# Attention weights of four heads turned together, and their sums with the values one piece later

## The chip, the cores and the metric

The kernel runs on one core of a Trainium2 chip. A time is the device time of one execution in microseconds (us); the kernel before was timed in three runs. One execution was also recorded instruction by instruction; times inside it count from the start of its span, the stretch from its first to its last instruction. Engines: TensorE (PE, matrix products; PEld is its loading of the stationary operand), VectorE (DVE), ScalarE (ACT), GpSimd (POOL), and SyncE (SP), which issues the loads of the weights.

## The reference

A decoder of two layers on 256 tokens of width 2048, all in float32. Layer 0 mixes by a state-space recurrence, layer 1 by attention; each is followed by a gated feed-forward part. The change touches the attention alone: 32 query heads of 64 columns, eight of them sharing one of four key/value heads, tokens in two blocks of 128, and each query sees at most the last 128 tokens:

```python
s = jnp.einsum('bnqhgd,bnkhd->bnhgqk', q, kw) * (HEAD_DIM ** -0.5)
s = s - slopes * dist
s = jnp.where(valid[None, :, None, None], s, -jnp.inf)
m = jnp.maximum(jnp.max(s, axis=-1, keepdims=True), sink)
p = jnp.exp(s - m)
p = p / (jnp.sum(p, axis=-1, keepdims=True) + jnp.exp(sink - m))
o = jnp.einsum('bnhgqk,bnkhd->bnqhgd', p, vw).reshape(bsz, seq, Q_DIM)
return (o @ w_o)
```

## The kernel before

**The large products.** Each weight matrix is read in blocks of 512 x 512, and each block is split into a high part (ScalarE, L122) and a low part (VectorE, L127). A *piece* (`piece`, with `products` at L922 to L924) multiplies one such block with the activations of 256 tokens: four quarters `a`, two token tiles `t`, three matmuls each (high x high, high x low, low x high), 24 matmuls into two accumulators named acc. `linear` runs the four pieces of one result of 512 columns. A piece asks for the weights that come three blocks later to be split, and for loads two further ahead.

**Work between pieces.** The list `slots` holds other work. After every piece `linear` takes the next entry of `slots` and issues all that is in it. Instructions go to their engines in the order that a scheduler chooses ahead of time: it follows the order of the code by priority, and puts later instructions of an engine ahead where it reckons that the earlier ones would wait. [...]

**Attention.** `attention` first computes keys and values (kv), then for each of four chunks c of eight heads the queries (a `linear`). `heads(c, q)` gives three functions for the chunk, each working on groups g4 of four heads:

- `turn_q` transposes the queries on TensorE (L1153) and copies them out.
- `scores(g4)` computes the scores of four heads (L1165 for the first token block, 128 columns; L1166 for the second, 256 columns), adds the slopes on VectorE (L1169), takes the maxima (L1170, L1171), exponentiates on ScalarE (L1181) and divides by the sums (L1187). A head's weights are 128 rows of 384 columns of the tile sc.
- `values(g4)` does for each head i: three transposes of 128 x 128 into one bank (L1197), a copy of that bank to the tile pT, on VectorE for even i and on ScalarE for odd i (L1199), and three matmuls with the values (L1208 to L1210) into half of a bank po: partitions 0 to 63 for an even head, 64 to 127 for an odd one. The sums of head i are issued after the transposes of head i + 1. After each odd head the bank is split into the high part (ScalarE, L1214) and the low part (VectorE, L1215) of oT, the left operand of the out-projection.

There are eight banks of matmul output (`ps`, bufs=8); `bank` takes one, for acc as for all tiles named here. pT has three buffers.

The slots of a chunk c are filled when its queries are issued, and worked off during the four pieces of the next `linear`: after the first piece turn_q, the second group's values of the chunk before, and scores(0); then scores(1); then values(0); then nothing. For chunk 3 they are worked off during the first eight pieces of the out-projection (order `O_ORDER`: its blocks of rows 0, 1, 2 for two accumulators each, then block 3 for both): turn_q with the late values and scores(0); scores(1); nothing; values(0); values(1). Block q of the out-projection reads the tile oT of chunk q, which is complete once both groups' values are done; block 3 is read from the seventh piece on.

## Time and profile before

| what | value |
|---|---|
| median of three runs | 2031.78 us (2030.18 to 2032.72) |
| the recorded execution | 2030.9 us |
| its span | 2029.1 us |
| TensorE busy in the span | 1984.3 us, 98% |
| VectorE, ScalarE busy | 1088.9 us, 860.1 us |
| mean granted TensorE clock | 0.993 |
| first to last start of a matmul with the values (L1208) | 1099.5 to 1230.0 us |

A line of a group of instructions reads: line in the code, engine, operation, tiles written <- tiles read, shapes, count | busy us, mean ns of one | idle us of that engine just before them, and what ended that idle time. A line of the timeline reads: start, duration, engine, line, operation, tiles, count, and in brackets the idle time ahead of it with what ended it; several of a kind are merged. Matmuls are pipelined, so their durations overlap, and one float32 matmul is recorded as one or two passes. "128*64" ahead of a shape is the part of TensorE's array (rows*columns) that the instruction uses.

### The profile page before, as it was taken

The page shows a single profiled execution, that of the slowest core. Times are in us where ns is not written, and L with a number is a line of the kernel's source. Part 1 is how long each engine was busy: PE and PEld are TensorE (multiplying, and loading weights), DVE is VectorE, ACT ScalarE, POOL GpSimd, SP SyncE. Part 2 cuts the span into 40 slices and gives each one's busy share as a digit, 9 for nine tenths or more (in the row PEclk, how much of TensorE's full clock was granted, in tenths as well). Part 3 has the DMA queues.
Part 4 walks back from the last instruction along what each step waited for, and adds up shares of the span by engine and source line. Part 5 has one row for each costly group of instructions (what it writes and reads, how often), then busy time and mean ns, then how long its engine had stood idle before and what let it go on. Part 6 is the DMA issues. An engine that isn't in the chain of part 4 may idle for free.

```text
span 2029.1 us, 25100 instructions
## 1 busy us (share of the span) xinstructions
PE 1984.3 (98%) x10640; PEld 1638.7 (81%) x10640; DVE 1088.9 (54%) x1343; ACT 860.1 (42%) x871; POOL 103.7 (5%) x77
## 2 busy tenths in 40 slices
PE   7699999999999999999999999999999999999998
PEld 6578888888888888888887778888888888888886
DVE  8955454445544544454567775544454445444445
ACT  6554444443344334333445454544333343334333
POOL 6850000000000000000000000000000000000000
PEclk9899999999999999999999999999999999999999
DMA  4037666565555655556555334556555655555564
GB/s 128 23 111 233 198 198 194 186 194 192 187 188 188 199 193 187 187 192 200 178 191 166 106 125 146 186 188 193 194 192 187 188 191 193 195 186 188 190 201 148
DMA packets 183317, 360.62 MB, mean 178 GB/s; under 512 B 10403, under 2 KB 10467, under 8 KB 183077
## 3 DMA queue, kind: packets, MB, share of 16 engines
q1 hardware_dynamic: 182192, 355.56, 54.4%
q8 instruction: 83, 1.36, 0.3%
q10 hardware_dynamic: 580, 2.14, 0.3%
q0 software_dynamic: 432, 1.33, 0.2%
q14 instruction: 30, 0.24, 0.0%
HBM read 356.90 MB, written 2.10 MB: 177 GB/s over the span
## 4 chain that ended last, share of the span: by engine, by line
PE 91%; DVE 6%; ACT 1%; DMA 1%; issue 1%; POOL 0%; DVEq 0%; ACTq 0%
PE acc L922 29%; PE acc L924 29%; PE acc L923 28%; DVE scan L573 1%; DVE w L127 1%; PE tr L1061 1%; DVE V L578 1%; DVE V L576 1%; DMA raw<-in_s_w_glu_dram 1%; PE pv L210 1%; PE tr L966 1%; PE po L1208 1%; PE tr L1197 0%; PE py L798 0%; ACT sc L1181 0%
## 5 line engine op out<-in xcount | busy, mean ns | idle before, releaser
L127 DVE TENSOR_TENSOR w<-raw,w 128x2048 fp32r<-128x2048 f32 x330 | 757.1, 2295 | 828.3 <-ACT w L122 828.3
L122 ACT ACTIVATE w<-raw 128x2048 fp32r<-128x2048 f32 x332 | 636.2, 1916 | 979.4 <-PE acc L924 873.6
L922 PE MATMUL acc<-w,xT 128*128 128x512 f32 x1568 | 612.8, 391 | 0.0
L924 PE MATMUL acc<-w,xT 128*128 128x512 f32 x1568 | 611.3, 390 | 0.0
L923 PE MATMUL acc<-w,xT 128*128 128x512 f32 x1568 | 610.6, 389 | 0.0
L924 PEld LDWEIGHTS acc<-w,xT 128*128 128x128 f32 x1568 | 294.3, 188 | 62.2 <-issue 1.0
L922 PEld LDWEIGHTS acc<-w,xT 128*128 128x128 f32 x1568 | 294.4, 188 | 61.3 <-issue 1.3
L923 PEld LDWEIGHTS acc<-w,xT 128*128 128x128 f32 x1568 | 294.4, 188 | 60.7 <-issue 0.5
L922 PE MATMUL acc<-w,hT 128*128 128x512 f32 x704 | 275.2, 391 | 0.0
L923 PE MATMUL acc<-w,hT 128*128 128x512 f32 x704 | 273.6, 389 | 0.0
L924 PE MATMUL acc<-w,hT 128*128 128x512 f32 x704 | 273.4, 389 | 0.0
L922 PEld LDWEIGHTS acc<-w,hT 128*128 128x128 f32 x704 | 132.1, 188 | 28.0 <-ACT hT L1063 1.2
L924 PEld LDWEIGHTS acc<-w,hT 128*128 128x128 f32 x704 | 132.1, 188 | 27.8
L923 PEld LDWEIGHTS acc<-w,hT 128*128 128x128 f32 x704 | 132.2, 188 | 27.0
L923 PE MATMUL acc<-w,gt 128*128 128x512 f32 x256 | 99.8, 390 | 0.6 <-DVE w L127 0.6
L922 PE MATMUL acc<-w,gt 128*128 128x512 f32 x256 | 100.1, 392 | 0.0
L924 PE MATMUL acc<-w,gt 128*128 128x512 f32 x256 | 99.7, 389 | 0.0
L923 PEld LDWEIGHTS acc<-w,gt 128*128 128x128 f32 x256 | 48.1, 188 | 10.6 <-DVE w L127 1.0
L924 PEld LDWEIGHTS acc<-w,gt 128*128 128x128 f32 x256 | 48.1, 188 | 10.1
L922 PEld LDWEIGHTS acc<-w,gt 128*128 128x128 f32 x256 | 48.1, 188 | 9.9
L1088 DVE TENSOR_TENSOR h<-h,acc 128x512 f32<-128x512 f32 x64 | 43.3, 686 | 23.7 <-PE acc L924 23.7
L1074 ACT ACTIVATE act<-acc,ry 128x512 f32<-128x512 f32 x44 | 30.1, 690 | 59.9 <-PE acc L924 59.9
(242 smaller groups left out, 1233.1 us busy)
## 6 DMA issues: line engine op xcount, KB each, us to landing
raw<-in_ffn_w_gate_dram SPq DMA_DIRECT2D x88, 1024.0 KB, 5.2
raw<-in_ffn_w_up_dram SPq DMA_DIRECT2D x88, 1024.0 KB, 5.2
raw<-in_ffn_w_down_dram SPq DMA_DIRECT2D x88, 1024.0 KB, 5.1
raw<-in_s_w_glu_dram SPq DMA_DIRECT2D x32, 1024.0 KB, 5.3
raw<-in_attn_w_qkv_dram SPq DMA_DIRECT2D x20, 1024.0 KB, 5.2
raw<-in_attn_w_o_dram SPq DMA_DIRECT2D x16, 1024.0 KB, 5.1
xk<-in_x_dram SPq DMA_DIRECT2D x4, 512.0 KB, 7.4
h<-in_x_dram SPq DMA_DIRECT2D x8, 256.0 KB, 5.6
```

What stands on the lines that cost most here:

```text
L122: keep(S.activation(w[:, 0], self.raw[i], AF.Copy))
L127: keep(e.tensor_tensor(lo, self.raw[i], hi.bitcast(F32), op=ALU.subtract))
L210: return (lambda *a, **k: pin(f(*a, **k))) if self.on else f
L573: keep(V.tensor_tensor(t_, ws[..., part], bc(Vt[hf][:, k - 1, :, part], 1, 2), op=ALU.mult))
L576: V.tensor_tensor(v, v, t_[:, 0], op=ALU.add)
L578: V.tensor_tensor(v, v, t_[:, 1, ::-1], op=ALU.add)
L922: keep(PE.matmul(acc, x_[:, 0], w[0][:, a], start=first, stop=False))
L923: PE.matmul(acc, x_[:, 0], w[1][:, a], start=False, stop=False)
L924: PE.matmul(acc, x_[:, 1], w[0][:, a], start=False, stop=last)
L966: PE.transpose(pt[:, t], h[t][:, kt * P : (kt + 1) * P], ident)
L1074: S.activation(s, pg[t], AF.Silu, scale=r[0][:, t : t + 1])
L1088: V.tensor_tensor(hc, hc, acc[t], op=ALU.add)
```

## The change

`values` is cut in two. `turned_s(g4)` transposes the weights of all four heads and copies them to four pT tiles (four buffers now, three before). `values(g4)` does only the sums, pair by pair of heads: a pair has one bank, and each of the three matmuls is issued first for the even head (partitions 0 to 63) and then for the odd one (64 to 127) before the next of the three.

The slots of a chunk become: after the first piece turn_q, turned_s of the second group of the chunk before, and scores(0); then values of that second group, and scores(1); then turned_s(0); then values(0). For chunk 3 two more slots follow, turned_s(1) and values(1); the empty slot there goes, so that values(1) comes after the sixth piece of the out-projection, where it came after the fifth.

```diff
-                def values(g4):
-                    s = st[g4]
-                    po = {}
-
-                    def turned(i):
+                def turned_s(g4):
+
+                    st["pT"] = []
+                    for i in range(4):
                         pt = bank([P, 3, P], "tr")
                         for b3 in range(3):
-                            PE.transpose(pt[:, b3], s[:, i, b3 * P : (b3 + 1) * P], ident)
-                        pT = ap.tile([P, 3, P], F32, tag="pT", name=nm("pT"), bufs=3)
+                            PE.transpose(pt[:, b3], st[g4][:, i, b3 * P : (b3 + 1) * P], ident)
+                        pT = ap.tile([P, 3, P], F32, tag="pT", name=nm("pT"), bufs=4)
                         (S.copy if i % 2 else V.tensor_copy)(pT, pt)
-                        return pT
...
-                    before = None
-                    for i in range(4):
-                        pT = turned(i)
-                        if before:
-                            weighted(*before)
-                        before = (i, pT)
-                    weighted(*before)
...
+                        st["pT"].append(pT)
+
+                def values(g4):
+
+                    v0, v1 = (kv[:, t, 256 + HD * c : 256 + HD * c + HD] for t in range(2))
+                    for i2 in range(2):
+                        po = bank([P, 2, P], "po")
+                        hs = [(po[e * HD : (e + 1) * HD], st["pT"][2 * i2 + e]) for e in range(2)]
+                        for o, pT in hs:
+                            PE.matmul(o[:, 0], v0, pT[:, 0], start=True, stop=True)
+                        for o, pT in hs:
+                            PE.matmul(o[:, 1], v0, pT[:, 1], start=True, stop=False)
+                        for o, pT in hs:
+                            PE.matmul(o[:, 1], v1, pT[:, 2], start=False, stop=True)
+                        a = 2 * g4 + i2
+                        v = po.rearrange("p t q -> p (t q)")
+                        S.copy(ot[c][:, 0, a], v)
+                        V.tensor_tensor(ot[c][:, 1, a], v, ot[c][:, 0, a].bitcast(F32), op=ALU.subtract)
...
-                turn_q, scores, values = heads(c, q)
-                slots.append([turn_q, *late, partial(scores, 0)])
-                slots.append([partial(scores, 1)])
-                if c == 3:
-                    slots.append([])
+                turn_q, scores, turned_s, values = heads(c, q)
+                slots.append([turn_q, *late[:1], partial(scores, 0)])
+                slots.append([*late[1:], partial(scores, 1)])
+                slots.append([partial(turned_s, 0)])
                 slots.append([partial(values, 0)])
-                late = [partial(values, 1)]
-                slots.append(late if c == 3 else [])
-
+                late = [partial(turned_s, 1), partial(values, 1)]
+            slots.extend([f] for f in late)
```

More of the change, by code (lines that the diff above doesn't have):

```diff
@@ L1199, in turned @@
                         (S.copy if i % 2 else V.tensor_copy)(pT, pt)
-                        return pT
-                    def weighted(i, pT):
-                        if i % 2 == 0:
-                            po[i // 2] = bank([P, 2, P], "po")
-                        rows = slice(i % 2 * HD, (i % 2 + 1) * HD)
-                        o = po[i // 2][rows]
-                        v0, v1 = (kv[:, t, 256 + HD * c : 256 + HD * c + HD] for t in range(2))
-                        PE.matmul(o[:, 0], v0, pT[:, 0], start=True, stop=True)
-                        PE.matmul(o[:, 1], v0, pT[:, 1], start=True, stop=False)
-                        PE.matmul(o[:, 1], v1, pT[:, 2], start=False, stop=True)
-                        if i % 2:
-                            a = 2 * g4 + i // 2
-                            v = po[i // 2].rearrange("p t q -> p (t q)")
-                            S.copy(ot[c][:, 0, a], v)
-                            V.tensor_tensor(ot[c][:, 1, a], v, ot[c][:, 0, a].bitcast(F32), op=ALU.subtract)
@@ L1217, in values @@
-                    before = None
-                    for i in range(4):
-                        pT = turned(i)
-                        if before:
-                            weighted(*before)
-                        before = (i, pT)
-                    weighted(*before)
-                return turn_q, scores, values
+                        st["pT"].append(pT)
[14 more added lines that the diff above has]
+                        V.tensor_tensor(ot[c][:, 1, a], v, ot[c][:, 0, a].bitcast(F32), op=ALU.subtract)
@@ L1227, in attention @@
+                return turn_q, scores, turned_s, values
             late = []
```

## The prediction

> **What bounds the kernel now.** I read the page first (busy time, the chain that ended last, the costliest groups), then the windows of the attention stage, then its groups by line, and last the timeline of TensorE alone, matmul by matmul. Two engines' lines and the chain settle the bound:

> ```profile
> PE 1984.3 (98%) x10640; PEld 1638.7 (81%) x10640; DVE 1088.9 (54%) x1343; ACT 860.1 (42%) x871; POOL 103.7 (5%) x77
> ...
> PE 91%; DVE 6%; ACT 1%; DMA 1%; issue 1%; POOL 0%; DVEq 0%; ACTq 0%
> L122 ACT ACTIVATE w<-raw 128x2048 fp32r<-128x2048 f32 x332 | 636.2, 1916 | 979.4 <-PE acc L924 873.6
> ```

> TensorE (PE) is busy nearly throughout and is 91% of the chain. The splitting of weights on ScalarE (L122) idles 979.4 us, 873.6 of it until a TensorE matmul gives a buffer back: weights wait for TensorE, not TensorE for weights. So a microsecond off TensorE's stream in the attention stage should come off the end, as long as nothing else becomes late there. In that stage VectorE (DVE) is the next engine. One query chunk c lasts exactly 37.16 us, from its first q transpose to the next chunk's:

> ```profile
> 1112.40:1149.56 37.16, 36.05 (x210) 27.98 (x208) 27.88 (x65) 18.96 (x48) 0.00 (x0) 1.00 0.34 114
> ```

> (columns: PE, PEld, DVE, ACT, POOL busy, then TensorE's granted clock, the DMA share, GB/s). VectorE is busy 27.88, ScalarE 18.96; the granted clock is 1.00 and the DMA share 0.34, so neither clock nor loads matter here.

> **What the touched instructions cost.** The groups by line over 1096 to 1231 us, where all the weighted sums with the values lie:

> ```profile
> L1197 PE MATMUL tr<-ident,sc 128*128 128x128 f32 x96 | 15.1, 281 | 0.0
> L1208 PE MATMUL po<-pT,kv 128*64 128x128 f32 x64 | 12.9, 298 | 4.0 <-DVE pT L1199 4.0
> L1215 DVE TENSOR_TENSOR oT<-po,oT 128x256 fp32r<-128x256 f32 x15 | 6.2, 415 | 9.5 <-ACT oT L1214 9.5
> L1214 ACT CAST oT<-po 128x256 fp32r<-128x256 f32 x16 | 5.9, 368 | 21.1 <-PE po L1210 21.1
> ```

> There are 96 transposes (32 heads of three) and, of each of the three matmuls of a head, 64 passes, that is two passes per matmul, six per head. Durations overlap in the pipeline, so I cost by starts. A matmul into acc starts every 0.23 us (three steps from 1133.33 to 1134.02, below); whatever lies between two of them beyond 0.23 is what the inserted work costs. The third group of four heads, on TensorE alone:

> ```profile
> 1132.21 0.39 PE L924 MATMUL acc<-w,xT 128*128 128x512 f32 x1
> 1132.44 0.82 PE L1197 MATMUL tr<-ident,sc 128*128 128x128 f32 x6
> 1133.02 0.47 PE L922 MATMUL acc<-w,xT 128*128 128x512 f32 x1
> 1133.33 0.39 PE L923 MATMUL acc<-w,xT 128*128 128x512 f32 x1
> ...
> 1134.02 0.39 PE L923 MATMUL acc<-w,xT 128*128 128x512 f32 x1
> 1135.52 0.43 PE L1208 MATMUL po<-pT,kv 128*64 128x128 f32 x2 [1.11 <-DVE pT L1199]
> ...
> 1137.89 0.48 PE L924 MATMUL acc<-w,xT 128*128 128x512 f32 x1
> 1138.21 0.39 PE L922 MATMUL acc<-w,xT 128*128 128x512 f32 x1
> ...
> 1139.60 0.39 PE L922 MATMUL acc<-w,xT 128*128 128x512 f32 x1
> 1139.92 0.43 PE L1208 MATMUL po<-pT,kv 128*64 128x128 f32 x2
> 1140.19 0.38 PE L1209 MATMUL po<-pT,kv 128*64 128x128 f32 x2
> 1140.40 0.38 PE L1210 MATMUL po<-pT,kv 128*64 128x128 f32 x2
> 1140.72 0.50 PE L923 MATMUL acc<-w,xT 128*128 128x512 f32 x1
> 1141.05 0.39 PE L924 MATMUL acc<-w,xT 128*128 128x512 f32 x1
> ```

> Six transposes cost 0.81 - 0.23 between their neighbours and 0.08 in the next, slower start: 0.66, so 0.11 each, with no price for going in and out. One head's sum, alone between acc matmuls, costs 1.12 - 0.23 + 0.10 = 0.99, though its six passes need only 0.66 at their 0.11 pitch (1140.19 to 1140.40 is two): 0.33 goes into changing from 128x128 tiles to 128x64 tiles and back. The stretch from 1134.02 to 1137.89 (two heads' sums, each followed by three transposes) costs 3.64 + 0.09 = 3.73, with a wait of 1.11 us for the turned weights' copy in it. With the fourth head, alone again behind it at the same 0.99, this group costs 0.66 + 3.73 + 0.99 + 0.99 = 6.4 us.

> I walked all eight groups of the TensorE timeline in this way (the one above is the third): 5.2, 4.3, 6.4, 4.3, 6.4, 4.3, 5.8, 4.5 us, together 41.2. That is everything the change touches on TensorE. The 4.0 us of waits of L1208 are inside it, in four groups.

> **Part by part.** *All four heads turned in one place* (turned_s): the same 12 transposes a group, no tile change among them: 12 x 0.11 = 1.32, eight times 10.6 us.

> *The sums one piece later* (values): they now follow 24 acc matmuls, 24 x 0.23 = 5.5 us, after the last transpose. The copy to pT was late by up to 1.1 us behind the cover of two to seven acc matmuls; 5.5 us is ample, so the 4.0 us of waits goes. All 24 passes of a group can then stand in one block, paying the tile change once in place of three or four times.

> *Two heads side by side.* Head 0 of a pair writes partitions 0 to 63 of the bank, head 1 partitions 64 to 127: two different 128x64 tiles of the array. The trace has such pairs already, where the scheduler happened to put two heads next to each other:

> ```profile
> 1103.14 0.40 PE L922 MATMUL acc<-w,xT 128*128 128x512 f32 x1
> 1103.47 0.43 PE L1208 MATMUL po<-pT,kv 128*64 128x128 f32 x2
> 1103.74 0.27 PE L1209 MATMUL po<-pT,kv 128*64 128x128 f32 x1
> 1103.74 0.32 PE L1208 MATMUL po<-pT,kv 128*64 128x128 f32 x1
> ...
> 1104.23 0.38 PE L1210 MATMUL po<-pT,kv 128*64 128x128 f32 x2
> 1104.54 0.50 PE L923 MATMUL acc<-w,xT 128*128 128x512 f32 x1
> 1104.88 0.39 PE L924 MATMUL acc<-w,xT 128*128 128x512 f32 x1
> ```

> Twelve passes cost 1.40 - 0.23 + 0.11 = 1.28, where two lone heads cost 1.98: they run at the same time, the second head's first pass 0.27 us after the first head's. In the new code each of the three matmuls is issued for both heads in turn, so the partner is third in the stream of passes and not seventh. I bound the lag by 0.05 (half the pitch) and by the 0.27 seen, and take 0.11, one pitch. A block of 24 passes then costs: 0.32 going in, 0.27 for the first two passes of a tile, 0.11 for each further start up to its twelfth (9 x 0.11 = 0.99), the lag of 0.11, 0.21 from the last start to the next acc matmul (1140.40 + 0.11 to 1140.72), less 0.23, plus 0.10: 1.77. Eight times: 14.2 us. With a lag of 0.05 it is 13.7, with 0.27 15.4; if the pairs only cost what the pair above did, 2 x 1.28 x 8 = 20.5.

> [...]

> *Copies and queues.* The copies to pT and the two instructions that end a pair (368 ns on ScalarE, 415 on VectorE) are as many as before; they issue no DMA, so the SP and POOL queues are passed by nothing. Those on ScalarE that sat 21.1 us waiting for L1210, holding up whatever is queued behind them, wait less, since their sums no longer wait. The added pT buffer costs no time. What lost cover: with chunk 3 the second group's sums now come after the sixth of the out-projection's eight pieces, straight ahead of the piece that reads them. That piece begins with two quarters from the first group, 12 x 0.23 = 2.8 us, and a pair's end takes 0.37 + 0.42 plus at worst one weight split on each engine (1.92 and 2.28): 5.0 us after the first pair, which is through about 0.7 us before the block's end, against 2.8 + 0.7 + 0.46 (the low part is read third) = 4.0. So 0 to 1.0 us, once.

> *The softmax ahead of the transposes.* The turning stays in the slot it had, except for chunk 3, where the empty slot goes. Scores to normalised weights took from 1119.72 (TensorE) to 1131.49 (VectorE):

> ```profile
> 1119.72 0.50 PE L1165 MATMUL at<-kT,qT 64*128 64x128 f32 x4
> ```
> ```profile
> 1129.57 1.92 DVE L1187 TENSOR_SCALAR sc<-sc,sm 128x128 f32<-128x128 f32 x8
> ...
> 1132.19 2.28 DVE L127 TENSOR_TENSOR w<-raw,w 128x2048 fp32r<-128x2048 f32 x1
> ...
> 1134.91 0.55 DVE L1199 COPY pT<-tr 128x384 f32<-128x384 f32 x1
> ```

> That is 11.8 us. Afterwards two pieces (11.0) and four heads' sums (1.8) lie between the scores and their turning: 12.8 us, without the scores' own matmuls. Covered by 1.0 us and those.

> **The sum.** 41.2 - 10.6 - 14.2 = 16.4 us less. I allow 1.0 us for waits in new places (the end of chunk 3, a bank now and then): 15.4. The profiled execution took 2030.9 us, 2015.5 then; the median of the runs is 0.9 above it, so I predict 2016.4. About 0.2% (4 us) is what a measurement can tell from no change.

> **Rivals.**
> *The blocks do not form, or pairs stay slow.* The program's scheduler orders each engine and put acc matmuls between heads in half the groups of before. If it still does between pairs, or the lag of 0.27 stays in each, a group costs up to 1.32 + 2.56: 31.1 us in all, a gain of 10.1, 7 if part of the 4.0 of waits stays. 2022 to 2025. For it: the gaps at 1138 and 1141. Against: those gaps stood where a copy was awaited, and now none is.

> *The turning waits for banks, and the kernel is slower.* There are eight banks. In the first slot of a chunk two acc, two for q and four for turned heads are eight, and four for scores follow; before, only two turned heads stood at once. A bank comes back when its copy is done, and VectorE's copy can sit behind a weight split: 2.28 + 0.55 = 2.83 us, as at 1132.19 and 1134.91. If each group paid that, 8 x 2.83 = 22.6 against the 16.4 gained: 6 us slower, 2038. It decides from 16.4 / 8 = 2.05 us per group on. [...] Against: L1197 shows 0.0 idle before it, and the first two copies, half of them on ScalarE, go on while the third and fourth head are turned. VectorE has 27.88 us of work for a chunk that would last 37.16 - (4.3 + 6.4 - 2 x 3.09) = 32.6: 85%, not full.

> *It does nothing measurable.* If the softmax became so much longer in VectorE's new order that TensorE waits 1.55 us or more before the turning of each group (past the 1.0 us of cover), eight times that takes 12.4 of the 16.4 away: 2028 to 2032.

> **Chances.** Forecast (2014 to 2020) 0.70; blocks broken or slow pairs (2020 to 2026) 0.17; nothing measurable 0.06; slower 0.07. Faster by over 0.2% is 0.87. The range runs from 2014.0 (lag 0.05, no new wait, and chunks 0 to 2 sharing the tile change with the scores behind them) to 2025.0, the slow pairs' end.

> **What would show it.** Right: eight blocks of L1208 to L1210, their starts about 0.055 us apart and first to last 1.3 to 1.4 us; L1197 in runs of 12; no wait of L1208 for pT; a chunk of about 32.6 us with VectorE at 27.9. Wrong: idle time before L1197 or L1165 released by a VectorE copy (banks), po in more than eight blocks, or wait before the acc matmuls that read oT.

## The result, and the profile after

The changed kernel takes 2014.45 us (median of 4 runs, 2013.38 to 2015.25) against 2031.68 us for the kernel before in the same job: 17.2 us less, a ratio of 0.9916 with a 95% interval of 0.9901 to 0.9932. The recorded execution took 2014.75 us, its span 2013.0. The busy times of its page:

```profile
PE 1971.2 (98%) x10640; PEld 1633.5 (81%) x10640; DVE 1087.0 (54%) x1343; ACT 857.9 (43%) x871; POOL 103.4 (5%) x77
```

There are as many matmuls as before (10640 records). The span is 16.1 us shorter: TensorE's idle time fell by 3.0 us (44.8 to 41.8) and its busy time by 13.1, since pairs that run side by side overlap, and overlapping records count once. One query chunk, from q transpose to q transpose (same columns as before):

```profile
1143.83:1176.35 32.52, 32.52 (x209) 26.55 (x208) 27.24 (x66) 18.44 (x48) 0.00 (x0) 1.00 0.37 130
```

32.52 us in place of 37.16, with the same work on VectorE (27.24 us busy, 27.88 before). The groups by line, now over 1096 to 1218 us:

```profile
L1196 PE MATMUL tr<-ident,sc 128*128 128x128 f32 x96 | 11.8, 272 | 0.0
L1208 PE MATMUL po<-pT,kv 128*64 128x128 f32 x64 | 6.6, 285 | 0.0
L1215 ACT CAST oT<-po 128x256 fp32r<-128x256 f32 x16 | 4.9, 358 | 0.0
```

The idle columns are empty: 4.0 us before L1208 and 21.1 before ScalarE's part of oT are gone, and the same 64 passes of L1208 keep TensorE busy for 6.6 us in place of 12.9. The third group of four heads on TensorE:

```profile
1129.62 0.39 PE L924 MATMUL acc<-w,xT 128*128 128x512 f32 x1
1129.86 1.47 PE L1196 MATMUL tr<-ident,sc 128*128 128x128 f32 x12
1131.08 0.48 PE L922 MATMUL acc<-w,xT 128*128 128x512 f32 x1
1131.40 0.40 PE L923 MATMUL acc<-w,xT 128*128 128x512 f32 x1
```
```profile
1136.43 0.39 PE L924 MATMUL acc<-w,xT 128*128 128x512 f32 x1
1136.75 0.44 PE L1208 MATMUL po<-pT,kv 128*64 128x128 f32 x4
...
1137.89 0.39 PE L1212 MATMUL po<-pT,kv 128*64 128x128 f32 x4
1138.21 0.50 PE L922 MATMUL acc<-w,xT 128*128 128x512 f32 x1
1138.55 0.40 PE L923 MATMUL acc<-w,xT 128*128 128x512 f32 x1
```

Four heads turned in one run of twelve, a piece of acc matmuls, then 24 passes in one block. "x4" merges two passes of each head; the trace has the partner's first pass 0.007 us behind the other's. By starts, the turning costs 1.23 + 0.09 us and the block 1.55 + 0.11 = 1.66.

**The yardstick of the stage.** For every kernel below I summed, from 1075 to 1245 us, by how much the distance of neighbouring acc matmuls exceeds their 0.227 us, wherever other work or a longer gap lay between them (the normalisation's transposes behind the attention, and the slower start right after them, left out). The kernel before gives 59.7 us (41.2 of it the turning and the sums, the rest queries and scores), the changed kernel 42.6: 17.1 us gained in this stage. The span shrank by 16.1 us only, because this execution entered the stage 0.94 us later; the tenth experiment is about that.

### The profile page after: what moved, and what is told of

It is laid out like the page before. It is cut to its first block, busy times and chain, and to the rows that moved or that the text cites. A ratio compares the mean times of both kernels' runs of the same rounds, so it can differ in the third digit from the quotient of the medians.

```text
span 2013.0 us, 25105 instructions
## 1 busy us (share of the span) xinstructions
PE 1971.2 (98%) x10640; PEld 1633.5 (81%) x10640; DVE 1087.0 (54%) x1343; ACT 857.9 (43%) x871; POOL 103.4 (5%) x77
## 4 chain that ended last, share of the span: by engine, by line
PE 93%; DVE 5%; DMA 1%; ACT 1%; issue 0%; POOL 0%; DVEq 0%; ACTq 0%
PE acc L922 29%; PE acc L924 29%; PE acc L923 29%; DVE scan L573 1%; PE tr L1061 1%; DVE V L578 1%; DVE V L576 1%; DMA raw<-in_s_w_glu_dram 1%; DVE w L127 1%; PE pv L210 1%; PE tr L966 1%; PE tr L1196 1%; PE py L798 0%; PE at L1166 0%; PE px L210 0%
## 5 line engine op out<-in xcount | busy, mean ns | idle before, releaser
L127 DVE TENSOR_TENSOR w<-raw,w 128x2048 fp32r<-128x2048 f32 x330 | 757.1, 2294 | 826.3 <-ACT w L122 826.2
L122 ACT ACTIVATE w<-raw 128x2048 fp32r<-128x2048 f32 x332 | 636.2, 1916 | 983.2 <-PE acc L924 834.1
L922 PE MATMUL acc<-w,xT 128*128 128x512 f32 x1568 | 613.1, 391 | 0.0
L924 PE MATMUL acc<-w,xT 128*128 128x512 f32 x1568 | 610.5, 389 | 0.0
L923 PE MATMUL acc<-w,xT 128*128 128x512 f32 x1568 | 610.2, 389 | 0.0
L922 PEld LDWEIGHTS acc<-w,xT 128*128 128x128 f32 x1568 | 294.4, 188 | 62.6 <-issue 2.3
L924 PEld LDWEIGHTS acc<-w,xT 128*128 128x128 f32 x1568 | 294.3, 188 | 61.5
L923 PEld LDWEIGHTS acc<-w,xT 128*128 128x128 f32 x1568 | 294.5, 188 | 60.3
L922 PE MATMUL acc<-w,hT 128*128 128x512 f32 x704 | 275.2, 391 | 0.0
L923 PE MATMUL acc<-w,hT 128*128 128x512 f32 x704 | 273.6, 389 | 0.0
L924 PE MATMUL acc<-w,hT 128*128 128x512 f32 x704 | 273.4, 389 | 0.0
L922 PEld LDWEIGHTS acc<-w,hT 128*128 128x128 f32 x704 | 132.2, 188 | 28.1 <-ACT hT L1063 1.2
L924 PEld LDWEIGHTS acc<-w,hT 128*128 128x128 f32 x704 | 132.1, 188 | 27.6
L923 PEld LDWEIGHTS acc<-w,hT 128*128 128x128 f32 x704 | 132.2, 188 | 27.0
L923 PE MATMUL acc<-w,gt 128*128 128x512 f32 x256 | 99.8, 390 | 0.6 <-DVE w L127 0.6
L922 PE MATMUL acc<-w,gt 128*128 128x512 f32 x256 | 100.1, 392 | 0.0
L924 PE MATMUL acc<-w,gt 128*128 128x512 f32 x256 | 99.7, 389 | 0.0
L923 PEld LDWEIGHTS acc<-w,gt 128*128 128x128 f32 x256 | 48.1, 188 | 10.8 <-DVE w L127 1.0
L924 PEld LDWEIGHTS acc<-w,gt 128*128 128x128 f32 x256 | 48.1, 188 | 10.0
L922 PEld LDWEIGHTS acc<-w,gt 128*128 128x128 f32 x256 | 48.1, 188 | 9.9
```

What stands on the lines that cost most here:

```text
L122: keep(S.activation(w[:, 0], self.raw[i], AF.Copy))
L127: keep(e.tensor_tensor(lo, self.raw[i], hi.bitcast(F32), op=ALU.subtract))
L922: keep(PE.matmul(acc, x_[:, 0], w[0][:, a], start=first, stop=False))
L923: PE.matmul(acc, x_[:, 0], w[1][:, a], start=False, stop=False)
L924: PE.matmul(acc, x_[:, 1], w[0][:, a], start=False, stop=last)
```

## The experiments

The stage column is the yardstick, the loss is against the changed kernel, first in the stage (one recorded execution each) and then by medians. The intervals of e1 and e7 overlap that of the changed kernel, and e9 and e10 are single runs: there the medians alone tell little, and the stage has to decide.

| run | us | ratio to before (95%) | stage | loss: stage, median |
|---|---|---|---|---|
| changed kernel | 2014.45 | 0.9916 (0.9901 to 0.9932) | 42.6 | |
| e1 head by head | 2016.54 | 0.9927 (0.9911 to 0.9943) | 44.7 | 2.1, 2.1 |
| e2 two heads by two | 2021.64 | 0.9950 (0.9936 to 0.9965) | 50.0 | 7.4, 7.2 |
| e3 full width | 2029.07 | 0.9986 (0.9977 to 0.9996) | 57.1 | 14.5, 14.6 |
| e4 no piece between | 2024.97 | 0.9965 (0.9952 to 0.9978) | 52.7 | 10.1, 10.5 |
| e6 no piece, head by head | 2026.35 | 0.9977 (0.9967 to 0.9986) | 55.7 | 13.1, 11.9 |
| e8 one bank held | 2019.92 | 0.9944 (0.9931 to 0.9958) | 47.7 | 5.1, 5.5 |
| e5 two banks held | 2022.54 | 0.9957 (0.9942 to 0.9973) | 49.7 | 7.0, 8.1 |
| e7 sums next to scores | 2015.35 | 0.9925 (0.9913 to 0.9938) | 43.9 | 1.3, 0.9 |
| e9 two matmuls in turn | 2014.82 (one run) | | 43.0 | 0.4, 0.4 |
| e10 changed kernel again | 2014.11 (one run) | | 42.6 | 0.0, -0.3 |

### Which order puts two heads side by side: e1, e2, e9

e1 issues the three matmuls of a head one after the other:

```diff
                         for o, pT in hs:
                             PE.matmul(o[:, 0], v0, pT[:, 0], start=True, stop=True)
-                        for o, pT in hs:
                             PE.matmul(o[:, 1], v0, pT[:, 1], start=True, stop=False)
-                        for o, pT in hs:
                             PE.matmul(o[:, 1], v1, pT[:, 2], start=False, stop=True)
```

> The changed kernel, but in each pair all three matmuls of the even head are issued before those of the odd head. My theory: passes of the other 128x64 tile overtake in TensorE's queue, and the partner only starts later, 0.27 us behind as in the pair at 1103 us of the kernel before, in place of 0.05: a block of 24 passes between acc matmuls costs 1.88 us in place of 1.66, 8 x 0.22 = 1.8 us in all, 2016.2 us. Rival (strict order of matmuls, so that only the issue order puts heads side by side): the heads run one after the other but for one pass, 24 x 0.11 + 0.33 = 2.97 a block, 8 x 1.3 = 10.5 us more, 2025 us.

The third group's block on TensorE in e1 (here L1209 and L1210 are a head's second and third matmul):

```profile
1136.20 0.39 PE L924 MATMUL acc<-w,xT 128*128 128x512 f32 x1
1136.52 0.43 PE L1208 MATMUL po<-pT,kv 128*64 128x128 f32 x2
1136.79 0.27 PE L1209 MATMUL po<-pT,kv 128*64 128x128 f32 x1
1136.79 0.32 PE L1208 MATMUL po<-pT,kv 128*64 128x128 f32 x1
...
1138.24 0.50 PE L922 MATMUL acc<-w,xT 128*128 128x512 f32 x1
```

2.04 - 0.23 = 1.81 us, with 0.11 in the next start 1.92 for the block against 1.66, eight times 0.26 = 2.1 us in all. The partner's first pass, seventh in the order of issue, starts with the third, both at 1136.79. My theory held (1.88 forecast; the rival's estimate was 2.97). The scheduler did not put the partner ahead: in the list of the built program for TensorE, the heads' matmuls stand in the order of the code in all eight blocks, in e1 as in e2 and e9. So in these runs it is TensorE that started them earlier.

e2 puts twelve passes ahead of the other tile:

```diff
...
+                    for e in range(2):
+                        for i2 in range(2):
+                            o, pT = po[i2][e * HD : (e + 1) * HD], st["pT"][2 * i2 + e]
...
```

> The changed kernel, but a group issues the sums of heads 0 and 2 (both in partitions 0 to 63) and then those of heads 1 and 3 (64 to 127): the other tile's first pass is the 13th of the block. My theory: overtaking with a lag that grows with the number of passes ahead, 0.27 us for six and so about 0.54 for twelve: a block costs 2.15 us in place of 1.66, 8 x 0.49 = 3.9 us more, 2018.4 us. Rival (strict order): the two tiles never run together, 2.97 a block, 2025 us. A second rival, that TensorE looks only some few passes ahead, gives a value between, with the second tile's first start close behind that of the first tile's 12th pass less the depth.

```profile
1137.38 0.39 PE L924 MATMUL acc<-w,xT 128*128 128x512 f32 x1
1137.70 0.43 PE L1208 MATMUL po<-pT,kv 128*64 128x128 f32 x2
...
1138.62 0.27 PE L1209 MATMUL po<-pT,kv 128*64 128x128 f32 x1
1138.63 0.32 PE L1208 MATMUL po<-pT,kv 128*64 128x128 f32 x1
...
1140.09 0.50 PE L922 MATMUL acc<-w,xT 128*128 128x512 f32 x1
```

The 13th pass (L1208 at 1138.63) starts with the ninth (L1209 at 1138.62), 0.93 us into the block; only the last four passes of the first tile run beside it, and the block costs 2.48 + 0.11 = 2.59 us. My lag of 0.54 us fell, the second rival held: the seventh pass started with the third in e1, the 13th 0.01 us behind the ninth in e2, each four places before its turn and ahead of the three passes between. e9 tests that where it should cost nothing, with the partner's first pass fifth:

```diff
                         for o, pT in hs:
                             PE.matmul(o[:, 0], v0, pT[:, 0], start=True, stop=True)
-                        for o, pT in hs:
                             PE.matmul(o[:, 1], v0, pT[:, 1], start=True, stop=False)
                         for o, pT in hs:
                             PE.matmul(o[:, 1], v1, pT[:, 2], start=False, stop=True)
```

> The changed kernel, but in each pair the first two matmuls of the even head, then the first two of the odd head, then the third of each: the other tile's first pass is the fifth of the block. Theory (TensorE starts a pass of the other tile up to four passes ahead: the seventh started with the third, the thirteenth with the ninth): the fifth starts with the first, 0.01 us behind, and a block costs 1.55 + 0.11 = 1.66 us as in the changed kernel; the time is the same, 2014.5 us within the 1 us of single runs. Rival (the lag grows with the passes ahead, 0.27 us for six, so 0.18 for four): a block of 1.84 us, 8 x 0.18 = 1.4 us more in the stage.

```profile
1136.36 0.39 PE L924 MATMUL acc<-w,xT 128*128 128x512 f32 x1
1136.68 0.45 PE L1208 MATMUL po<-pT,kv 128*64 128x128 f32 x4
...
1138.19 0.50 PE L922 MATMUL acc<-w,xT 128*128 128x512 f32 x1
```

All four first passes merge into one row at 1136.68: the fifth starts with the first, as forecast. The block is 1.60 + 0.11 = 1.71, 0.05 over the changed kernel and not the rival's 1.84. The 0.05 comes from the second pair, whose partner falls 0.06 us behind.

### What side by side is worth: e3

```diff
...
-                        po = bank([P, 2, P], "po")
-                        hs = [(po[e * HD : (e + 1) * HD], st["pT"][2 * i2 + e]) for e in range(2)]
...
+                    for i in range(4):
+                        po = bank([P, 2, P], "po")
+                        pT = st["pT"][i]
+                        PE.matmul(po[:, 0], vv[:, 0], pT[:, 0], start=True, stop=True)
...
```

> The changed kernel, but the sums use the whole 128x128 array: the values stand twice side by side in the stationary operand (a copy by GpSimd), each head has a bank of its own, and only its half of the rows is copied on (twice as many copies, of half the rows). No tile change and no heads side by side, and no wait for pT. My theory (side by side halves the block, the tile change costs 0.33): 24 x 0.11 = 2.64 + 0.1 a block against 1.66, or against 1.46 where scores follow: 5 x 1.1 + 3 x 1.3 = 9.3 us more, 2023.8 us. Rival (the gain came from the waits and the tile changes alone): within 2 us of the changed kernel, 2016 us at most.

The block alone came out as forecast, 24 passes at 0.11 without a tile change, between the acc matmuls at 1139.12 and 1141.94, 2.82 - 0.23 + 0.09 = 2.68 us:

```profile
1139.12 0.39 PE L924 MATMUL acc<-w,xT 128*128 128x512 f32 x1
...
1141.94 0.48 PE L922 MATMUL acc<-w,xT 128*128 128x512 f32 x1
1142.26 0.39 PE L923 MATMUL acc<-w,xT 128*128 128x512 f32 x1
```

The other 5.2 us of the loss I had not forecast. They lie mostly in the three places where scores follow the sums. The sums take four banks instead of two, and twice as many copies empty them; the scores then wait for a bank:

```profile
1161.33 0.48 PE L1165 MATMUL at<-kT,qT 64*128 64x128 f32 x2 [0.24 <-DVE oT L1218]
...
1163.62 0.48 PE L1165 MATMUL at<-kT,qT 64*128 64x128 f32 x2 [0.25 <-DVE oT L1218]
```

The third and fourth head's scores each wait for VectorE to empty a bank; they no longer run side by side, and acc matmuls of the scheduler's choice stand between them. This run does not separate the number of banks from the number of copies. The rival (within 2 us) is refuted by the block alone: side by side, after paying for the tile change that full width does without, is worth 2.68 - 1.66 = 1.0 us a group. At full width the first pass starts 0.23 us after the last acc matmul (1139.12 to 1139.35), in the changed kernel 0.32 us (1136.43 to 1136.75).

### What the piece between is worth: e4, e6

```diff
-                slots.append([turn_q, *late[:1], partial(scores, 0)])
-                slots.append([*late[1:], partial(scores, 1)])
-                slots.append([partial(turned_s, 0)])
-                slots.append([partial(values, 0)])
+                slots.append([turn_q, *late, partial(scores, 0)])
+                slots.append([partial(scores, 1)])
+                if c == 3:
+                    slots.append([])
+                slots.append([partial(turned_s, 0), partial(values, 0)])
                 late = [partial(turned_s, 1), partial(values, 1)]
-            slots.extend([f] for f in late)
+                slots.append(late if c == 3 else [])
```

> The changed kernel with its sums right behind the turning in one slot, in the slots of the kernel before; heads side by side and turned in one place as changed. My theory (the piece between hides the copies to pT): TensorE waits for pT again, about 1.1 us in half of the groups, and the scheduler breaks blocks by acc matmuls, 0.33 us each time, in some six places: 4.4 + 2.0 = 6.4 us more, 2020.9 us. Rival (the scheduler fills the wait anyway, the place is indifferent): 1 us at most, 2015.5 us.

In the waits of TensorE, e4 has 3.9 us for pT in four places again. The third group:

```profile
1135.09 0.43 PE L1208 MATMUL po<-pT,kv 128*64 128x128 f32 x2 [1.14 <-DVE pT L1198]
1135.45 0.50 PE L924 MATMUL acc<-w,xT 128*128 128x512 f32 x1
1135.79 0.40 PE L922 MATMUL acc<-w,xT 128*128 128x512 f32 x1
1136.12 0.32 PE L1208 MATMUL po<-pT,kv 128*64 128x128 f32 x1
```

One matmul of the even head comes first, then two acc matmuls while the odd head's copy is awaited, then twelve passes, and the last ten only at 1140 us. In all, the sums lie in 22 stretches, where the changed kernel has 8 and the kernel before had 18. So the wait came out nearly as forecast (3.9 us, 4.4 forecast), and the breaks were underrated: 14 more stretches in place of six, and 10.1 - 3.9 = 6.2 us for them. That is 0.44 each, an average of what is left over and not a price measured at one break. e6 is e4 with the head-by-head order of e1:

> Sums right behind the turning in one slot, as in the run without the piece between, and the three matmuls of a head issued before those of the next head. My theory: with the sums waiting for copies, side by side costs rather than helps, since a pair can only go on when both copies are there; head by head, the first head's six passes start as soon as its own copy is done, so blocks break less: 1 to 3 us less than with pairs and no piece between, 2022 to 2024 us. Rival (the order within a pair is worth its 2.1 us here too): 2 us more, 2027 us.

My theory fell; in the stage the rival held. There are fewer stretches (16), but the waits are the same (3.9 us), and the stage loses another 3.0 us: the order within a pair is worth 2.1 us with the piece between and 3.0 without. By medians e6 loses 1.4 us against e4, with overlapping intervals; the stage is the cleaner measure.

Together, in the stage: turning four heads in one place alone (the kernel before to e6) is worth 4.0 us; the piece between 11.0 (e6 to e1) or 10.1 (e4 to the changed kernel); the order of the pairs 2.1 (e1 to the changed kernel) or 3.0 (e6 to e4). Either way from the kernel before to the changed one adds up to 17.1.

### Whether banks limit it: e8, e5

```diff
+            held = [bank([P, P], "held") for _ in range(1)]
+            for b_ in held:
+                PE.transpose(b_, ident, ident)
...
+            for b_ in held:
+                V.tensor_tensor(nd[:, :P], nd[:, :P], b_, op=ALU.add)
```

> As the run with two banks held, with one held: seven banks for everything. My theory (the changed kernel just has enough banks): a part of the loss with two, 2 to 6 us more, 2016.5 to 2020.5 us. Rival (banks are no limit): none, 2014.5 us.

> The changed kernel with two of the eight banks taken through the attention (two more transposes at its start, two small additions after the last scores read them): six banks for everything, and two beside the four accumulators once the out-projection has begun. My theory (banks are what limits four heads at once, and the changed kernel just has enough): TensorE waits for VectorE's and ScalarE's copies before the third and fourth turned head and before the scores, 1 to 2 us in each of eight groups, 8 to 16 us more, 2022 to 2030 us. Rival (copies come back in time, the banks are no limit; the split scores of the full-width run came from twice the copies): 1.5 us at most, 2016 us.

Both times lie in the bands of the theory, e5 at the edge of its band, but the loss has another form than the theory gave it: only in part a wait. With one bank less, half of the 5.1 us (three places of 0.83) is this, the end of the scores behind the second q transposes:

```profile
1150.89 0.40 PE L923 MATMUL acc<-w,xT 128*128 128x512 f32 x1
1151.21 0.49 PE L1168 MATMUL at<-kT,qT 64*128 64x128 f32 x2
1151.54 0.59 PE L1169 MATMUL at<-kT,qT 64*128 64x256 f32 x2
1152.06 0.50 PE L924 MATMUL acc<-w,xT 128*128 128x512 f32 x1
1152.40 0.40 PE L922 MATMUL acc<-w,xT 128*128 128x512 f32 x1
```

The fourth head's scores have become a stretch of their own: 1.17 - 0.23 + 0.11 = 1.05 us, with no idle time of TensorE in it. The scheduler put acc matmuls where the bank would be lacking, and the price is the additional tile change and the lost partner. The other half (three places of 0.81) is in blocks that stay whole. There the fourth head's scores, behind the sums, wait for VectorE to give a bank back, 0.4 us each time by the weight loads (PEld), and no longer run beside the third's:

```profile
PEld at L1168 <- DVE sc L1172: 1.2, 3, 0.4
```

With two banks held, one turning also waits 1.1 us for a copy to pT, as the theory said; the rest of the 7.0 us is in broken or held-up scores as in e8. So eight banks suffice for the changed kernel, and seven do not.

### A version that might beat it: e7

```diff
+                if c in (1, 2):
+                    slots.append([turn_q, late[0], partial(scores, 0)])
+                    slots.append([late[1]])
+                    slots.append([late[2], partial(scores, 1)])
...
+                late = [partial(values, 0), partial(turned_s, 1), partial(values, 1)]
```

> The changed kernel with its slots dealt out anew for chunks 1 and 2: queries turned, sums of the first group of the chunk before, first scores; turning of the second group; its sums and the second scores; turning of the first group. Both groups' sums then lie next to scores. Theory: each block of sums next to scores costs 1.46 us, not 1.66, and the first scores no longer wait for the copies of the queries (0.3 us): 2 x 0.5 = 1.0 us less, 2013.4 us. Rival (the scheduler or VectorE makes up for it by a new wait, as the second scores come only a piece later than the second turning needs them): the same or up to 3 us slower, 2014.5 to 2017.5 us.

The interval overlaps that of the changed kernel, and the stage is 1.3 us longer. The rival held: TensorE now waits 0.9 us for the queries ahead of L1153 and, with chunk 2's sums too close ahead of the piece that reads them, 0.3 us for oT. Of the theory's two gains one came: the first scores of chunks 1 and 2 cost 1.71 us again. The other did not, as the scheduler put acc matmuls between the first group's sums and the scores. None of these runs beats the changed kernel.

### What belongs to the change and what to the execution: e10

> The changed kernel itself once more. Theory: the attention stage repeats to 0.1 us, and the 0.9 us by which the first recorded execution entered it later than the kernel before comes from the first layer and differs from execution to execution. Rival: the 0.9 us is there again and belongs to the change.

The first q transposes of the kernel before, the changed kernel, and the changed kernel again:

```profile
1080.53 1.03 PE L1153 MATMUL tr<-ident,q 128*128 128x128 f32 x8
```
```profile
1081.47 1.03 PE L1153 MATMUL tr<-ident,q 128*128 128x128 f32 x8
```
```profile
1080.84 1.03 PE L1153 MATMUL tr<-ident,q 128*128 128x128 f32 x8
```

0.94 us later once, 0.31 the second time; the stage itself gave 42.61 and 42.62 us. My theory held: the stage's 17.1 us belongs to the change, and what comes ahead varied by up to a microsecond between these three executions.

## Why the prediction was right

**The bound.** TensorE's stream was the bound, and a microsecond off it in the attention came off the end: 17.1 us in the stage, 17.2 by medians. Behind the attention, from the normalisation's first transpose to the end, both recorded executions take 779.3 us.

**The sum.** Forecast 41.2 - 10.6 - 14.2 - 1.0 = 15.4; measured 41.2 - 10.6 - 12.7 - 0.9 = 17.0. Term by term:

- *Turning:* 8 x (1.23 + 0.09) = 10.6 us, as forecast.
- *Sums:* 5 blocks of 1.66 and 3 of 1.46 that share the tile change with the scores behind them, 12.7 us, where I had 14.2. The mis-sized term is the lag of the partner: I took 0.11 us between 0.05 and 0.27, and it is 0.007, below both bounds. That is 0.8 us over eight blocks. The rest is the shared change, which I had left to the range. So the result lies near the low end of the range, 2 us under the point.
- *Waits in new places:* none in the places I named. L1196 and L1208 wait for nothing, and chunk 3's last sums are followed at once by the piece that reads them. What I did not see: the first scores, now right behind twenty transposes, cost more than the 1.71 us that they cost alone or behind sums.

```profile
1143.60 0.39 PE L924 MATMUL acc<-w,xT 128*128 128x512 f32 x1
1143.83 1.09 PE L1153 MATMUL tr<-ident,q 128*128 128x128 f32 x8
1144.75 1.47 PE L1196 MATMUL tr<-ident,sc 128*128 128x128 f32 x12
1146.16 0.48 PE L1165 MATMUL at<-kT,qT 64*128 64x128 f32 x2
1146.51 0.48 PE L1166 MATMUL at<-kT,qT 64*128 64x256 f32 x1
1146.52 0.49 PE L1165 MATMUL at<-kT,qT 64*128 64x128 f32 x2
...
1148.02 0.50 PE L922 MATMUL acc<-w,xT 128*128 128x512 f32 x1
```
```profile
1144.07 1.92 ACT L122 ACTIVATE w<-raw 128x2048 fp32r<-128x2048 f32 x1 [3.59 <-PE acc L924]
1145.89 0.56 ACT L1154 COPY qT<-tr 128x512 f32<-128x512 f32 x1
```

4.42 - 0.23 - 20 x 0.109 = 2.01 us: the second head's scores start 0.36 us behind the first's, not beside them. Three such places make 0.9 us. The lower rows show what they wait for: ScalarE's copy of the second token block of the queries, which L1166 reads. It comes behind the split of a weight and ends at 1146.46 us; L1166 starts 0.05 us later, as it does behind that copy in the other two places. In e7, where the sums lie between, the copy is long done and the scores cost 1.71 us again. So this is a wait in a new place after all, though the page counts it as no idle time of TensorE. That its 0.9 us so nearly fills the 1.0 I had allowed for other places is luck.

**The steps.** Right: eight blocks, runs of twelve transposes, no wait for pT, a chunk of 32.5 us (32.6 forecast) with VectorE's work unchanged. The softmax is in time, as L1196 waits for nothing. The piece between does hide the copies (e4), and it does more than that: it lets the 24 passes stand together, which is worth more than the 3.9 us of waits (6.2 of the 10.1 us that e4 loses).

**The rivals.** The blocks did form. Nor did strict order, the rival in e1 and e2, hold: in the kernel before, the second head's first pass starts at 1103.74 with the first head's third, in e1 the seventh pass with the third (1136.79), in e2 the 13th with the ninth (1138.63 and 1138.62). So the alternating order itself, which e1's rival put at 10.5 us, is worth only 2.1 us of the 17.1. Banks did not limit the changed kernel, but e8 and e5 show that the rival stood one bank away, and that its form would have been another: not waits of 2.83 us for a copy in every group, but scores that the scheduler splits or that wait 0.4 us for a bank and lose their partner, 5.1 us with one bank less.

## What to carry to other kernels

Put a whole piece of other work between the copy of a small product's operand and its use. Here that saved not only the wait: the product's passes then stood in one block, while in e4 the scheduler filled the wait with other matmuls, and the breaks cost 6.2 us beside it (0.44 us each on average). Two products in different 128x64 tiles ran side by side from the start of the block when the other one's first pass was issued third or fifth (0.007 and 0.01 us behind the first); strict alternation bought 0.4 us in the stage beyond that (e9). Look also at what now follows right behind the moved work: here the first scores met a copy that sums had covered before (0.9 us in three places). And before giving work more banks at a time, count them: here eight suffice and seven cost 5.1 us, and much of the loss shows as broken blocks and lost partners rather than as idle time.
